# Router of the second norm in each of two encoder layers: from the normed rows to the residual sum, half a tile at a time

## The chip, the cores and the metric

The kernel runs on one core of a Trainium2 chip. The metric is device time in microseconds (us) of one execution, as the median of several runs. Engines are named as in the profile: PE is TensorE (matmul), PEld its weight loads, DVE is VectorE, ACT is ScalarE, POOL is GpSimd, SP is the engine that issues most DMAs.

## The reference

Two post-norm encoder layers on 1024 tokens of width 1024. Only the place around the second norm and the router matters here:

```python
x = layer_norm(DN_ALPHA * x + y, ln2_g[l], ln2_b[l])       # y: cross-attention's output
y = expert_choice_moe(x, moe_router[l], w_gate[l], w_up[l], w_down[l])

def expert_choice_moe(x, w_router, w_gate, w_up, w_down):
    cap = EC_FACTOR * n_tok // N_EXPERTS                   # 128
    aff = jax.nn.softmax((x @ w_router).astype(jnp.float32), axis=-1)   # (tokens, 16)
    gates, idx = lax.top_k(aff.transpose(0, 2, 1), cap)    # each expert takes its 128 best tokens
    xe = jax.vmap(lambda xb, ib: xb[ib])(x, idx)           # gather
    ...                                                    # SwiGLU, scatter-add
```

## The kernel before

Tokens are cut into eight tiles of 128 rows. The function `proj_ln` (L1170 on) does the output projection of cross-attention and the second norm. Its loop (L1188) takes one tile per step `t`; each step has 16 slots `i` of three products (a product of split fp32r halves: high by high, high by low, low by high), 48 products of 512 columns in all. After slot 7 the first half of the row, and after slot 15 the second, is added to the scaled residual (`add`, L1201, on DVE, with the statistics of that half, L1135). Then `layer_norm` (L1138) forms mean and variance (L1144), the root on ACT (L1146), two passes of 1024 columns on DVE (L1148, L1154) and the reciprocal. The normed tile is handed to `emit2`, which writes `x2d` and `yd` to DRAM through ACT's queue.

The router runs as a side thread, a generator `tg` that is moved on at fixed slots. `turned2` transposes the normed tile on PE in two groups of four blocks (L1463), each group is taken out of PSUM by ACT (high part, L175) and DVE (low part, L176); then 16 short products against the router weights `rw` (L1482) give 16 logits twice (for the two parts), ACT copies them (L1484), PE turns them (L1487), DVE adds the two (L1489), and the softmax follows (L1492 to L1497). A tile's two groups are transposed at slots 9 and 10 of the next step, its products come at slot 0 of the step after that and its softmax at slot 6 there.

A second side thread, `bg`, ranks the affinities on DVE: `rank` sorts the scores of four tiles once tile 3's softmax is done, then of two tiles once tile 5's is done. It is moved on by one yield per slot up to slot 8 of the last step, and 11 more yields follow it after the last step, between the pieces of the last tile's router. `route` then ranks the last two tiles (26 yields), with one yield of `bg` behind each of its own as long as `bg` has any; from the threshold it makes two masks, counts tokens by products with a triangle and with ones (L1583 to L1588), and gives every expert its list. Expert 0's rows are gathered (L1651), transposed (L1463), and the first expert product follows. The experts' weights are loaded through SP's queue into a pool of 41 buffers that is shared with everything else.

PE, ACT and DVE execute in the order in which the program is written. SP and POOL are ordered by a planner.

`router_weights` (L1468) loads the 1024 by 16 router weights and splits them; it stands between the last turn of the first norm's rows and the first full products of cross-attention on PE.

Of the kernel before, what the change touches and what calls it, by code (L numbers as in the profile page):

```python
# [11 lines left out]
F32 = mybir.dt.float32  # L12
# [51 lines left out]
R4 = 4  # L64
ST = lambda nc: nc.scalar
YB = 1
EARLY = {4: 1, 5: 2, 6: 2, 7: 6, 8: 5}

FWD = ((0, 2), (4, 6), (1, 3), (5, 7))
# [68 lines left out]
class Net:  # L138
# [58 lines left out]
    def consts(self):  # L197
        nc, cp, A = self.nc, self.cp, self.A
        self.ident = cp.tile([128, 128], F32, name="ident")
        nc.sync.dma_start(self.ident, A["k_ident"])  # L200
        self.eps = cp.tile([128, 2], F32, name="eps")
        nc.vector.memset(self.eps[:, 0:1], 1e-6)
        nc.vector.memset(self.eps[:, 1:2], 1e-5)
        self.x1d = [self.dp.tile([N, D], F32, name=f"x1d{l}") for l in range(DEPTH)]
# [927 lines left out]
    def stats(self, r, st, i):  # L1132
# [2 lines left out]
        self.nc.vector.bn_stats(st[:, i, :], r[:, i * 512:i * 512 + 512])  # L1135
        return st

    def layer_norm(self, r, g, b, split=False, st=None, src=None):  # L1138
# [4 lines left out]
        mv = self.sml(2, "mv")  # L1143
        nc.vector.bn_aggr(mv, st.rearrange("p a b -> p (a b)"))  # L1144
        sd = self.sml(1, "lsd")
        nc.scalar.activation(sd, mv[:, 1:2], AF.Sqrt, bias=self.eps[:, 1:2], scale=1.0)  # L1146
# [23 lines left out]
    def proj_ln(self, raw, ws, res, g, b, emit, turned, per=2, bg=iter(())):  # L1170


        nc = self.nc
        ws[0].get()
        HL = {0: self.split_pair(raw, 0)}
        ws[1].get()
        g = self.bcast(g, 1024, "lng")
        b = self.bcast(b, 1024, "lnb")
        rs = {}

        def load(t):
            rs[t] = self.big(name="r")
            nc.sync.dma_start(rs[t], res[t * 128:(t + 1) * 128, :])

        load(0)
        yield
        done, tg = [], iter(())
        for t in range(NT + 2):  # L1188
            if per == 2:
                tg = turned((t - 3) // 2) if t % 2 and t >= 3 else iter(())  # L1190
            if t < NT:
                if t + 1 < NT:
                    load(t + 1)
                P = [self.psS((128, 512)) for _ in range(2)]
                H, L = HL[t // 2]
                d = slice((t % 2) * 128, (t % 2) * 128 + 128)
                r, st = rs.pop(t), None

                def add(n):
                    c = slice(n * 512, n * 512 + 512)  # L1200
                    nc.vector.scalar_tensor_tensor(r[:, c], r[:, c], ALPHA, P[n], op0=OP.mult, op1=OP.add)  # L1201
                    return self.stats(r, st, n)

                for i in range(16):
                    n, k = divmod(i, 8) if t else (i % 2, i // 2)
# [15 lines left out]
            if per == 2 or t >= NT:  # L1221
# [12 lines left out]
            if t < NT:  # L1234
                for n in range(bool(t), 2):
                    st = add(n)
                self.layer_norm(r, g, b, LS(per, t), st)
                done.append((t, r))
            yield
# [226 lines left out]
            yield  # L1466

    def router_weights(self, l):  # L1468
        nc = self.nc
        raw = self.cp.tile([128, 8, 16], F32, name="rt", tag="rt")  # L1470
        nc.sync.dma_start(raw, self.A["moe_router"][l].rearrange("(k p) e -> p k e", p=128))
        w = self.cp.tile([128, 8, 32], F32R, name="rw", tag="rw")
        self.split(w[:, :, 0:16], w[:, :, 16:32], raw)
        return w

    def router(self, w, X, t):

        nc = self.nc
        P = self.psO((128, 128))
# [4 lines left out]
        nc.scalar.activation(lg[0:32], P[0:32], AF.Copy)  # L1484
        yield
        P = self.psT((128, 2, 16))
        nc.tensor.transpose(P.rearrange("p a e -> p (a e)"), lg[0:32], self.ident[0:32, 0:32])  # L1487
        s = self.sml(16, "rlg")
        nc.vector.tensor_reduce(s, P.rearrange("p a e -> p e a"), axis=AX.X, op=OP.add)  # L1489
        e = self.aff[:, t, 0:16]  # L1490
        nm = self.sml(1, "rnm")
        nc.vector.tensor_reduce(nm, s, axis=AX.X, op=OP.max, negate=True)  # L1492
        sm = self.sml(1, "rsm")
        nc.scalar.activation(e, s, AF.Exp, bias=nm, scale=1.0, accum_out=sm)
# [56 lines left out]
    def route(self, bg):  # L1551
# [28 lines left out]
            nc.vector.tensor_tensor(M[:, j], aff, tb.unsqueeze(1).to_broadcast([128, 8, 16]), op)  # L1580
        C = self.psT((128, 2, 8, 16))
        mm, tri, one = nc.tensor.matmul, self.tri[:, 0, :], self.tri[:, 1, :]
        mm(C, tri, M, start=True, stop=False)  # L1583
# [173 lines left out]
    def run(self):  # L1757
# [38 lines left out]
        for l in range(DEPTH):  # L1796
# [54 lines left out]
            wo2 = []  # L1851
            rw = self.router_weights(l)
            T2 = self.new_T()
            st2 = {}

            def emit2(t, x):
                self.tap(f"x2_{l}_{t}", x)
# [4 lines left out]
                st2[t] = x  # L1862

            def turned2(t):
                X = [self.big((128, 8, 128), F32R, name="xt") for _ in range(2)]
                yield from self.turn_tile(st2.pop(t), *X, TL(t))
                yield from self.router(rw, X, t)
                self.ranked += 1
                yield
# [166 lines left out]
```

## Time and profile before

| what | us |
|---|---|
| median of 3 runs (2730.67 to 2734.1) | 2730.91 |
| the profiled execution | 2730.33 |
| its span, first to last instruction | 2728.6 |

How to read it: the page gives busy time per engine, the chain of work that ended last, and groups of instructions by line. The trace gives rows in order of time: start, duration, engine, line, operation, what is written and read, and in brackets how long the engine was idle before it and what released it. An engine that never waits sets the time of its stretch; an engine that is idle while others are done is waiting on the chain. The stage in question runs from about 930 us to 1077 us for layer 0, and once more for layer 1.

### The profile page before, as it was taken

The page shows a single profiled execution, that of the slowest core. Times are in us where ns is not written, and L with a number is a line of the kernel's source. Part 1 is how long each engine was busy: PE and PEld are TensorE (multiplying, and loading weights), DVE is VectorE, ACT ScalarE, POOL GpSimd, SP SyncE. Part 2 cuts the span into 40 slices and gives each one's busy share as a digit, 9 for nine tenths or more (in the row PEclk, how much of TensorE's full clock was granted, in tenths as well). Part 3 has the DMA queues.
Part 4 walks back from the last instruction along what each step waited for, and adds up shares of the span by engine and source line. Part 5 has one row for each costly group of instructions (what it writes and reads, how often), then busy time and mean ns, then how long its engine had stood idle before and what let it go on. Part 6 is the DMA issues. An engine that isn't in the chain of part 4 may idle for free.

```text
span 2728.6 us, 39209 instructions
## 1 busy us (share of the span) xinstructions
PE 2540.0 (93%) x14132; PEld 2138.4 (78%) x14132; DVE 1963.7 (72%) x3089; ACT 1589.2 (58%) x2828; POOL 830.0 (30%) x761
## 2 busy tenths in 40 slices
PE   7899989999999895999989998999989999599998
PEld 5688879988778784777869887999877888477775
DVE  6765578877645678889876556887765356889887
ACT  4743379988123443887854425998732344377885
POOL 2412427963101201121131333688230130011112
PEclk9899999999999996999999999999999999799999
DMA  7545100333233357999975610005323235699994
GB/s 196 192 161 200 28 24 17 75 100 120 86 109 118 121 187 252 351 378 371 342 241 171 208 60 24 9 24 140 94 85 101 85 101 185 239 340 372 377 344 154
DMA packets 222581, 462.76 MB, mean 170 GB/s; under 512 B 26298, under 2 KB 83216, under 8 KB 222386
## 3 DMA queue, kind: packets, MB, share of 16 engines
q1 hardware_dynamic: 198402, 374.56, 39.2%
q0 software_dynamic: 19376, 68.91, 9.5%
q10 hardware_dynamic: 4608, 16.78, 1.5%
q8 instruction: 111, 1.82, 0.3%
q14 instruction: 84, 0.69, 0.1%
HBM read 369.75 MB, written 90.44 MB: 169 GB/s over the span
## 4 chain that ended last, share of the span: by engine, by line
PE 70%; DVE 13%; issue 5%; ACT 5%; DMA 4%; POOL 2%; SPq 0%; ACTq 0%; DVEq 0%; POOLq 0%
PE S L187 7%; PE S L188 7%; PE S L189 7%; PE S L527 6%; PE O L1709 6%; PE T L544 5%; PE O L189 5%; PE O L188 5%; PE O L187 5%; PE S L421 4%; PE O L555 3%; PE O L554 3%; DVE rk L1512 2%; DMA eg<-moe_w_up 1%; PE T L1463 1%
## 5 line engine op out<-in xcount | busy, mean ns | idle before, releaser
L176 DVE TENSOR_TENSOR egl<-eg,egh 128x1024 fp32r<-128x1024 f32 x256 | 305.8, 1221 | 49.9 <-ACT egh L175 45.6
L530 DVE TENSOR_REDUCE nm<-S 128x1 f32<-128x1024 f32 x192 | 234.5, 1223 | 102.5 <-PE S L527 100.4
L175 ACT ACTIVATE egh<-eg 128x1024 fp32r<-128x1024 f32 x256 | 265.1, 1058 | 41.0 <-PE S L188 23.9
L176 DVE TENSOR_TENSOR PL<-T,PH 128x512 fp32r<-128x512 f32 x384 | 246.3, 683 | 17.4 <-ACT PH L175 14.2
L175 ACT ACTIVATE PH<-T 128x512 fp32r<-128x512 f32 x384 | 209.4, 595 | 69.0 <-PE T L544 67.6
L536 ACT ACTIVATE E<-S,nm 128x1024 f32<-128x1024 f32 x192 | 214.7, 1118 | 7.7 <-DVE nm L530 7.4
L187 PE MATMUL S<-woh,mh 128*128 128x512 f32 x512 | 207.9, 406 | 6.0 <-DVE r L1201 6.0
L544 PE MATMUL T<-ident,E 128*128 128x128 f32 x1536 | 203.4, 274 | 2.3 <-DVE PL L176 1.4
L188 PE MATMUL S<-wol,mh 128*128 128x512 f32 x512 | 202.1, 395 | 3.7 <-POOL wol L176 2.4
L544 PEld LDWEIGHTS T<-ident,E 128*128 128x128 f32 x1536 | 179.7, 141 | 32.2 <-DVE PL L176 4.0
L187 PE MATMUL S<-egh,xt 128*128 128x512 f32 x512 | 204.1, 399 | 0.0
L189 PE MATMUL S<-woh,ml 128*128 128x512 f32 x512 | 201.6, 394 | 0.0
L189 PE MATMUL S<-egh,xt 128*128 128x512 f32 x512 | 200.9, 392 | 0.0
L188 PE MATMUL S<-egl,xt 128*128 128x512 f32 x512 | 200.6, 392 | 0.0
L176 DVE TENSOR_TENSOR edl<-ed,edh 128x1024 fp32r<-128x1024 f32 x128 | 153.2, 1220 | 18.5 <-ACT edh L175 18.5
L1709 PE MATMUL O<-edh,ht 128*128 128x512 f32 x512 | 155.4, 406 | 1.4 <-ACT ht L175 1.4
L527 PE MATMUL S<-KS,QS 128*128 128x512 f32 x512 | 148.1, 413 | 1.6 <-ACT E L536 1.6
L1651 POOL DMA_INDIRECT xg<-x2d,ix x32 | 54.6, 1705 | 301.0 <-PE O L1709 143.0
L175 ACT ACTIVATE edh<-ed 128x1024 fp32r<-128x1024 f32 x128 | 132.4, 1055 | 22.8 <-PE S L188 13.2
L569 POOL TENSOR_TENSOR olo<-olo 64x256 f32<-64x256 f32 x96 | 70.3, 733 | 227.3 <-ACT olo L567 185.3
L554 PE MATMUL O<-PH,VS 128*128 128x256 f32 x512 | 137.9, 302 | 0.0
L1724 POOL DMA_INDIRECT yd<-ye,ix x31 | 49.1, 1583 | 260.9 <-ACT ye L1723 104.8
(438 smaller groups left out, 7093.1 us busy)
## 6 DMA issues: line engine op xcount, KB each, us to landing
eg<-moe_w_gate SPq DMA_DIRECT2D x128, 512.0 KB, 11.2
eg<-moe_w_up SPq DMA_DIRECT2D x128, 512.0 KB, 11.2
ed<-moe_w_down SPq DMA_DIRECT2D x128, 512.0 KB, 11.4
wv<-xa_wkv SPq DMA_DIRECT2D x16, 512.0 KB, 8.0
wk<-xa_wkv SPq DMA_DIRECT2D x16, 512.0 KB, 6.3
wo<-w_o SPq DMA_DIRECT2D x16, 512.0 KB, 3.5
x1d<-r SPq DMA_DIRECT2D x16, 512.0 KB, 2.6
wq<-xa_wq SPq DMA_DIRECT2D x16, 512.0 KB, 4.2
```

Source lines behind the costliest of these rows:

```text
L175: self.nc.scalar.activation(h, src, AF.Copy)
L176: (self.nc.vector if le == "v" else self.nc.gpsimd).tensor_sub(l, src, h.bitcast(F32))
L187: mm(out, ah, bh, start=start, stop=False)
L188: mm(out, ah, bl, start=False, stop=False)
L189: mm(out, al, bh, start=False, stop=stop)
L421: nc.tensor.matmul(P[:, hf * 512:hf * 512 + 512], a[:, k, :], self.half(b, hf, k), start=s, stop=e)
L527: self.nc.tensor.matmul(S[:, hf * 512:hf * 512 + 512], a, b[hf], start=n == 0, stop=n == len(passes) - 1)
L530: self.nc.vector.tensor_reduce(nm, S, axis=AX.X, op=OP.max, negate=True)
L536: self.nc.scalar.activation(E, S, AF.Exp, bias=nm, scale=1.0, accum_out=den)
L544: self.nc.tensor.transpose(pt[:, k, :], P[:, kt * 128:(kt + 1) * 128], self.ident)
L554: nc.tensor.matmul(O[:, :256], v, PH[half][:, k, :], start=kt == 0, stop=False)
L1709: nc.tensor.matmul(O[e][n], a[:, 2 * u + f, :], w[:, n * 512:n * 512 + 512], start=s, stop=z)
```

## The change

- `router_weights` also loads the norm's gain and bias, multiplies the router weights with them on POOL (gain in place, bias into a new tile), and takes the column sums of both over the 1024 inputs with 16 products of 16 columns each whose stationary operand is a 128 by 128 block of ones in fp32.
- The router takes the residual sum `r` in place of the normed row. The two groups are turned at slot 12 of the tile's own step (first half) and at slot 3 of the next step; the products are at slot 6 and the softmax at slot 9 of the next step. The mean and the reciprocal root are brought in afterwards, with two small DVE passes on 16 columns.
- For tiles 4 to 7 the turned rows stay whole fp32 (ACT alone takes them out of PSUM) and eight fp32 products with 16 columns of weights replace 16 split ones. Tiles 0 to 3 keep the split.
- The normed row goes into a tile of its own, `x2`. For the last tile the second pass of the norm stands behind the router's softmax; two yields of `bg` stand in the tail in place of 11.
- In `route` the counting products are seven with the moving operand shifted by a tile (both masks in one), and one over a sum of the first mask, which DVE forms, in place of 14 and 8.

```diff
+RF = lambda t: t >= 4
@@ proj_ln
-                    if per == 1 and i == TK(t)[0]:
-                        tg = turned(t - 1) if t else tg
-                    if per == 1 and i in TK(t) or per == 2 and i % 4 == 3 and t + 1 < NT:
+                    if per == 1 and i == 12 and t:
+                        drain(tg)
+                        tg = turned(t, r)
+                    if per == 1 and (i in (3, 6, 9, 12) and t or i == 2 and t == 1) or per == 2 and i % 4 == 3 and t + 1 < NT:
                         next(tg, None)
...
-            if per == 1 and t == NT:
-                tg = turned(t - 1)
-                for n in BGL:
-                    for _ in range(n):
-                        next(bg, None)
-                    next(tg, None)
-                drain(tg)
             if t < NT:
                 for n in range(bool(t), 2):
                     st = add(n)
+            if per == 1 and t == 0:
+                tg = turned(t, r)
+            if per == 1 and t < NT:
+                x = self.big(name="x2")
+                mv, sd = self.moments(st)
+                rs_ = self.sml(1, "lrs")
+                if t == NT - 1:
+                    next(tg)
+                    nc.vector.reciprocal(rs_, sd)
+                    nc.vector.scalar_tensor_tensor(x, r, mv[:, 0:1], g, op0=OP.subtract, op1=OP.mult)
+                    self.moment[t] = mv, rs_
+                    next(tg)
+                    next(bg, None)
+                    next(bg, None)
+                    drain(tg)
+                    nc.vector.scalar_tensor_tensor(x, x, rs_, b, op0=OP.mult, op1=OP.add)
+                    emit(t, x)
...
@@ router_weights
+        bw = self.tmp((128, 8, 16), name="rbw")
+        nc.gpsimd.tensor_tensor(bw, raw, gb[:, 1].unsqueeze(2).to_broadcast([128, 8, 16]), OP.mult)
+        nc.gpsimd.tensor_tensor(raw, raw, gb[:, 0].unsqueeze(2).to_broadcast([128, 8, 16]), OP.mult)
...
+        P = self.psO((128, 2, 16))
+        for i, x in enumerate((raw, bw)):
+            for k in range(8):
+                nc.tensor.matmul(P[:, i], self.one.to_broadcast([128, 128]), x[:, k], start=k == 0, stop=k == 7)
@@ router
+            if len(X) == 1:
+                nc.tensor.matmul(P[0:16], whole[:, k, :], X[0][:, k, :], start=k == 0, stop=k == 7)
+                continue
...
+        mv, rs = self.moment.pop(t)
+        u = self.sml(16, "rlg")
+        nc.vector.scalar_tensor_tensor(u, c[:, 0], mv[:, 0:1], s, op0=OP.mult, op1=OP.subtract)
+        nc.vector.scalar_tensor_tensor(u, u, rs, c[:, 1], op0=OP.mult, op1=OP.subtract)
@@ route
-        for t in range(NT):
-            for j in range(2):
-                if t < NT - 1:
-                    mm(C[:, j, t + 1:], one, M[:, j, t:t + 1].to_broadcast([128, NT - 1 - t, 16]), start=False, stop=False)
-            mm(C[:, 1], one, M[:, 0, t:t + 1].to_broadcast([128, NT, 16]), start=False, stop=t == NT - 1)
+        for d in range(1, NT):
+            mm(C[:, :, d:], one, M[:, :, 0:NT - d], start=False, stop=False)
+        mm(C[:, 1], one, above.unsqueeze(1).to_broadcast([128, NT, 16]), start=False, stop=True)
```

## Rows read from the trace of the kernel before

**Rows 1.** The page: the chain that ended last, by engine; the 128x512 eviction.
```profile
PE 70%; DVE 13%; issue 5%; ACT 5%; DMA 4%; POOL 2%; SPq 0%; ACTq 0%; DVEq 0%; POOLq 0%
L175 ACT ACTIVATE PH<-T 128x512 fp32r<-128x512 f32 x384 | 209.4, 595 | 69.0 <-PE T L544 67.6
```
**Rows 2.** Busy time by window: PE, PEld, DVE, ACT, POOL, granted clock, DMA share, GB/s.
```profile
1020.00:1035.00 15.00, 14.27 (x77) 11.24 (x76) 13.72 (x50) 5.93 (x11) 0.00 (x0) 1.00 0.78 274
1050.00:1060.00 10.00, 0.00 (x0) 0.00 (x0) 9.74 (x72) 0.00 (x0) 1.56 (x4) 0.50 1.04 402
```
**Rows 3.** Waits of PE from 925 to 1036 us, two lines of three.
```profile
PE S L187 <- DVE r L1201: 0.8, 1, 0.8
PE T L1463 <- DVE rlg L1489: 0.7, 1, 0.7
```
**Rows 4.** Timeline of PE in one undisturbed step: start, duration, engine, line, shapes.
```profile
949.66 0.60 PE L1463 MATMUL T<-ident,r 128*128 128x128 f32 x4
950.01 0.48 PE L187 MATMUL S<-woh,mh 128*128 128x512 f32 x1
...
955.34 1.12 PE L1482 MATMUL O<-xt,rw 128*32 128x128 f32 x16
956.30 0.44 PE L187 MATMUL S<-woh,mh 128*128 128x512 f32 x1
```
**Rows 5.** Whole fp32 products of 512 columns at the end: timeline, then the line's instructions.
```profile
2698.91 1.88 PE L1959 MATMUL S<-r,ident 128*128 128x512 f32 x4
...
L1959 PE MATMUL S<-r,ident x32: 590/592/697, 2695.2 to 2718.0; 128*128 128x512 f32 x32
```
**Rows 6.** Timeline of PE: eight short fp32 products, and the long product behind them.
```profile
810.61 1.03 PE L1403 MATMUL T<-ident,xE 128*128 128x128 f32 x8
811.40 0.48 PE L187 MATMUL O<-xh,wqh 128*128 128x512 f32 x1
```
**Rows 7.** Timeline of the tail of layer 0, from the last projection product on.
```profile
1035.30 1.17 PEld L1482 LDWEIGHTS O<-xt,rw 128*32 128x32 f32 x16
...
1037.51 0.29 ACT L1146 ACTIVATE lsd<-mv,eps 128x1 f32<-128x1 f32 x1 [1.60 <-DVE mv L1144]
1037.71 0.25 ACT L1484 ACTIVATE lg<-O 32x128 f32<-32x128 f32 x1
1037.97 1.28 ACT L1494 ACT_TABLE_LOAD   x1
...
1047.39 0.31 ACT L1494 ACTIVATE aff<-rlg,rnm 128x16 f32<-128x16 f32 x1 [1.09 <-DVE rnm L1492]
...
1048.29 0.24 DVE L1524 STREAM_TRANSPOSE rk<-aff 128x64 f32<-128x64 f32 x1
```
**Rows 8.** Timeline of DVE in the ranking: two threads in turn, then one alone.
```profile
1053.24 1.97 DVE L1512 TENSOR_TENSOR rk<-rk 128x32 f32<-128x32 f32 x16
...
1061.90 1.49 DVE L1512 TENSOR_TENSOR rk<-rk 32x64 f32<-32x64 f32 x8
```
**Rows 9.** Timeline: first counting product, and DVE's first work on the counts.
```profile
1065.14 0.40 PE L1583 MATMUL T<-rM,trib 128*128 128x256 bf16 x1 [0.80 <-DVE rM L1580]
...
1067.20 0.29 DVE L1591 SCALAR_TENSOR_TENSOR rk<-T,rM 128x128 f32<-128x128 f32 x1 [2.12 <-PE T L1588]
```
**Rows 10.** Timeline of DVE: the next pair split, a norm's second pass, a ranking's first step.
```profile
992.53 1.88 DVE L176 TENSOR_TENSOR ml<-xo,mh 128x512 fp32r<-128x512 f32 x3
...
997.81 1.28 DVE L1154 SCALAR_TENSOR_TENSOR r<-r,lrs,lnb 128x1024 f32<-128x1024 f32 x1
...
1002.04 0.31 DVE L1524 STREAM_TRANSPOSE rk<-aff 128x128 f32<-128x128 f32 x1
```
**Rows 11.** The first gather, and DMA by window just before it.
```profile
1070.78 1.04 POOL L1651 DMA_INDIRECT xg<-x2d,ix  x1 [19.01 <-DVE ix L1617]
...
1064.00:1065.00 1.00, 0.28 (x1) 0.17 (x1) 0.59 (x4) 0.00 (x0) 0.00 (x0) 0.50 0.40 152
```
**Rows 12.** SP's queue at the kernel's start: six loads of single values.
```profile
16.55 3.09 SPq L343 DMA_DIRECT2D cw<-hy_conv_w  x6
```

More of the change, by code (lines that the diff above doesn't have):

```diff
@@ L203, in consts @@
         nc.vector.memset(self.eps[:, 1:2], 1e-5)
+        self.one = cp.tile([128, 1], F32, name="one")
+        nc.vector.memset(self.one, 1.0)
         self.x1d = [self.dp.tile([N, D], F32, name=f"x1d{l}") for l in range(DEPTH)]
@@ L1136, in stats, with moments @@
         return st
+    def moments(self, st):
+        mv = self.sml(2, "mv")
+        self.nc.vector.bn_aggr(mv, st.rearrange("p a b -> p (a b)"))
+        sd = self.sml(1, "lsd")
+        self.nc.scalar.activation(sd, mv[:, 1:2], AF.Sqrt, bias=self.eps[:, 1:2], scale=1.0)
+        return mv, sd
     def layer_norm(self, r, g, b, split=False, st=None, src=None):
@@ L1142, in layer_norm @@
             st = self.stats(src, self.stats(src, None, 0), 1)
[L1143 to L1146, printed above, removed]
+        mv, sd = self.moments(st)
         rs = self.sml(1, "lrs")
@@ L1220, in proj_ln @@
                         st = add(0)
-            if per == 2 or t >= NT:
+            if per == 2 or t > NT:
                 drain(tg)
@@ L1236, in proj_ln @@
                     st = add(n)
+            if per == 1 and t == 0:
+                tg = turned(t, r)
+            if per == 1 and t < NT:
+                x = self.big(name="x2")
+                mv, sd = self.moments(st)
+                rs_ = self.sml(1, "lrs")
[10 more added lines that the diff above has]
+                    emit(t, x)
+                else:
+                    nc.vector.scalar_tensor_tensor(x, r, mv[:, 0:1], g, op0=OP.subtract, op1=OP.mult)
+                    nc.vector.reciprocal(rs_, sd)
+                    self.moment[t] = mv, rs_
+                    nc.vector.scalar_tensor_tensor(x, x, rs_, b, op0=OP.mult, op1=OP.add)
+                    done.append((t, x))
+            elif t < NT:
                 self.layer_norm(r, g, b, LS(per, t), st)
@@ L1468, in router_weights @@
     def router_weights(self, l):
-        nc = self.nc
+        nc, A = self.nc, self.A
         raw = self.cp.tile([128, 8, 16], F32, name="rt", tag="rt")
-        nc.sync.dma_start(raw, self.A["moe_router"][l].rearrange("(k p) e -> p k e", p=128))
+        nc.sync.dma_start(raw, A["moe_router"][l].rearrange("(k p) e -> p k e", p=128))
+        gb = self.cp.tile([128, 2, 8], F32, name="rgb", tag="rgb")
+        for i, k in enumerate(("ln2_g", "ln2_b")):
+            nc.sync.dma_start(gb[:, i], A[k][l].rearrange("(k p) -> p k", p=128))
+        bw = self.tmp((128, 8, 16), name="rbw")
+        nc.gpsimd.tensor_tensor(bw, raw, gb[:, 1].unsqueeze(2).to_broadcast([128, 8, 16]), OP.mult)
+        nc.gpsimd.tensor_tensor(raw, raw, gb[:, 0].unsqueeze(2).to_broadcast([128, 8, 16]), OP.mult)
         w = self.cp.tile([128, 8, 32], F32R, name="rw", tag="rw")
         self.split(w[:, :, 0:16], w[:, :, 16:32], raw)
-        return w
+        P = self.psO((128, 2, 16))
+        for i, x in enumerate((raw, bw)):
+            for k in range(8):
+                nc.tensor.matmul(P[:, i], self.one.to_broadcast([128, 128]), x[:, k], start=k == 0, stop=k == 7)
+        c = self.cp.tile([128, 2, 16], F32, name="rc", tag="rc")
+        nc.scalar.activation(c, P, AF.Copy)
+        return w, raw, c
     def router(self, w, X, t):
         nc = self.nc
+        w, whole, c = w
+        n = 16 if len(X) == 1 else 32
         P = self.psO((128, 128))
         for k in range(8):
+            if len(X) == 1:
+                nc.tensor.matmul(P[0:16], whole[:, k, :], X[0][:, k, :], start=k == 0, stop=k == 7)
+                continue
             for a in range(2):
@@ L1483, in router @@
         lg = self.tmp((128, 128), name="lg")
-        nc.scalar.activation(lg[0:32], P[0:32], AF.Copy)
+        nc.scalar.activation(lg[0:n], P[0:n], AF.Copy)
         yield
[L1486 to L1489, printed above, removed]
+        P = self.psT((128, n))
+        nc.tensor.transpose(P, lg[0:n], self.ident[0:n, 0:n])
+        if n == 16:
+            s = P
+        else:
+            s = self.sml(16, "rlg")
+            nc.vector.tensor_reduce(s, P.rearrange("p (a e) -> p e a", a=2), axis=AX.X, op=OP.add)
+        mv, rs = self.moment.pop(t)
+        u = self.sml(16, "rlg")
+        nc.vector.scalar_tensor_tensor(u, c[:, 0], mv[:, 0:1], s, op0=OP.mult, op1=OP.subtract)
+        nc.vector.scalar_tensor_tensor(u, u, rs, c[:, 1], op0=OP.mult, op1=OP.subtract)
         e = self.aff[:, t, 0:16]
         nm = self.sml(1, "rnm")
-        nc.vector.tensor_reduce(nm, s, axis=AX.X, op=OP.max, negate=True)
+        nc.vector.tensor_reduce(nm, u, axis=AX.X, op=OP.min)
         sm = self.sml(1, "rsm")
-        nc.scalar.activation(e, s, AF.Exp, bias=nm, scale=1.0, accum_out=sm)
+        nc.scalar.activation(e, u, AF.Exp, bias=nm, scale=-1.0, accum_out=sm)
         ri = self.sml(1, "rri")
@@ L1582, in route @@
         mm, tri, one = nc.tensor.matmul, self.tri[:, 0, :], self.tri[:, 1, :]
+        above = self.tp.tile([128, 16], BF16, tag="olo", name="rab", bufs=2)
+        with nc.allow_low_precision("counts up to 8"):
+            nc.vector.tensor_reduce(above, M[:, 0].rearrange("p t e -> p e t"), axis=AX.X, op=OP.add)
         mm(C, tri, M, start=True, stop=False)
-        for t in range(NT):
-            for j in range(2):
-                if t < NT - 1:
-                    mm(C[:, j, t + 1:], one, M[:, j, t:t + 1].to_broadcast([128, NT - 1 - t, 16]), start=False, stop=False)
-            mm(C[:, 1], one, M[:, 0, t:t + 1].to_broadcast([128, NT, 16]), start=False, stop=t == NT - 1)
+        for d in range(1, NT):
+            mm(C[:, :, d:], one, M[:, :, 0:NT - d], start=False, stop=False)
+        mm(C[:, 1], one, above.unsqueeze(1).to_broadcast([128, NT, 16]), start=False, stop=True)
         yield
@@ L1853, in run @@
             T2 = self.new_T()
-            st2 = {}
+            self.moment = {}
             def emit2(t, x):
@@ L1861, in emit2, with turned2 @@
                 ST(nc).dma_start(self.yd[l][t * 128:(t + 1) * 128, :], y)
[L1862 to L1866, printed above, removed]
+            def turned2(t, r):
+                if RF(t):
+                    X = [self.big((128, 8, 128), name="xt")]
+                    for c in range(2):
+                        pt = self.psT((128, 4, 128))
+                        for k in range(4):
+                            j = c * 4 + k
+                            nc.tensor.transpose(pt[:, k, :], r[:, j * 128:(j + 1) * 128], self.ident)
+                        nc.scalar.activation(X[0][:, c * 4:c * 4 + 4, :], pt, AF.Copy)
+                        yield
+                else:
+                    X = [self.big((128, 8, 128), F32R, name="xt") for _ in range(2)]
+                    yield from self.turn_tile(r, *X, TL(t))
                 yield from self.router(rw, X, t)
```

## The prediction, made before the changed kernel was run

> **What bounds the kernel now.** I read the chain of waits first: by engine PE has 70% of it and DVE 13% [rows 1]. So in most stages an instruction added on PE is paid, and the stage around this change may be one of the DVE stretches. The windows tell the two apart. From 1020 to 1035 us, inside the last projection steps, PE is busy 14.27 of 15 us at the full clock, and DVE 13.72 of 15: PE ends last, with DVE close behind. From 1050 to 1060 PE does nothing, the granted clock is 0.50 and DVE is busy 9.74 of 10 [rows 2]. So a step lasts as long as its PE work, and from the last projection product until the lists are made, the chain is the router of tile 7, then the ranking on DVE, then the counts. The timeline of that tail gives its parts: last product 1035.30, ranking of tiles 6 and 7 from 1048.29 [rows 7], counting products from 1065.14 [rows 9], gather 1070.78 [rows 11]. The waits say how far PE already waits for DVE in the steps: 0.8 and 0.7 us [rows 3], little beside eight steps. Layer 1 repeats all of it, so each term below is paid twice.
>
> **A. Column sums, on PE.** New work where PE runs without a pause, at the start of cross-attention. Each fp32 product appears as two records: the 16 products of 512 columns on the last stage are 32 records [rows 5]. So 16 products are 32 records, each with a 128-column fp32 stationary and 16 moving columns. No row has that shape. The nearest is eight fp32 records with 128 stationary and 128 moving columns, which hold PE 0.79 us, 0.10 each [rows 6]; 32 of them are 3.2, with 0.1 of fill **+3.3**. Bounds: the sixteen router records take 0.96, 0.06 each [rows 4], so 1.9; above, 0.12 each if the short stream hides nothing of a load, 3.9. POOL's multiplications, the extra small evictions and DVE's column pass lie long before they are used; I cost them at nothing. Without that cover they would delay the first router, by under 1 us.
>
> The row shows 0.10 per record with 128 moving columns, which doesn't tell whether the stationary or the moving side sets it. [...]
>
> **B. PE work ahead of the last projection product.** Tiles 4, 5 and 6 now have their fp32 products inside the steps; before, the split products of tiles 4 and 5 were there and tile 6's came behind the last product. An fp32 record of 512 columns takes (1.88 - 0.59) / 3 = 0.43 [rows 5], so one of 128 columns 0.1075, and a tile, eight products, 16 records, 1.72. A split tile takes 0.96 [rows 4]. 3 x 1.72 - 2 x 0.96 = 3.24; one more group's fill and turn of logits, 0.5 (an estimate from the 0.35 that four transposes take [rows 4]); the first half of tile 7 turned before the end, 0.35 and 0.1 of fill. **+4.2**. The bounds are 0.06 per record (then 0.96 a tile, +1.9) and 4.7.
>
> **C. DVE and the slots.** The first ranking starts when tile 3's softmax is through: now at 1002.04, in step 5 [rows 10]; after the change at slot 9 of step 4, the step in which DVE also splits halves of the next pair (1.88) [rows 10]. DVE's row sum then comes late, and the second half of tile 4, turned at slot 3, waits at PE, behind which the projection's products are queued: about 1.5 (an estimate: half of DVE's added 3 us is taken up by slots that have slack). For tiles 0 to 3 the products wait for the low half that DVE makes only three slots earlier; 0.2 a tile, 0.8. Of the 1.5 of waits now [rows 3] I take off 1.1, as the reasons shift but part recurs. **+1.2**. Bounds: -1.1 (no new wait) and +3 (the whole of DVE's addition).
>
> **D. Last product to ranking: 13.0 now** (1048.29 - 1035.30) [rows 7]. After: the root starts 2.2 behind the product as now and ends at 2.5 [rows 7]; ACT takes the second half out of PSUM, 0.6 [rows 1], 3.1; fp32 products 1.72 with a small fill, 4.9; logits 0.25, 5.2; then the table load, 1.28 [rows 7], under which the turn and the small DVE passes lie, 6.4; from the exponential to the ranking 0.9 [rows 7], 7.3; and the second pass of the norm, 1.28 [rows 10], ahead of it on DVE, 8.6. **-4.3**. What goes is the wait for the whole normed row before the turns, and nine yields of the other ranking. Bounds: -2.6 if the clock is already at half for the fp32 products (1.72 more), -4.8 if ACT takes the half out ahead of the root.
>
> **E. Ranking.** Where two rankings take turns DVE does 16 operations in 1.97, where one is alone 8 in 1.49 [rows 8]: two operations a yield cost 0.25 beside another and 0.37 alone, the rest hidden delay. By my count of yields 18 of the other thread are left beside this one, not 22: four fewer pairs of 0.54, four more of 0.37, **-0.7** (0 to -1.2). **F. Counts.** 23 products of 2176 columns lie in 2.06 us at the half clock [rows 9]; 1280 columns in nine products: **-0.7** (-0.3 to -0.9). DVE's sum over the tiles lies beside the first products.
>
> **Other.** Two more loads of single values at the kernel's start, each like one of the six (0.5) [rows 12], on SP ahead of others: +0.3 once, at most 1. Tile 7's normed row is written 1.3 us later, still ahead of the gather. SP's load of layer 1's router weights now waits for layer 0's last fp32 router, and SP's later loads stand behind it; those are hundreds of microseconds ahead of use.
>
> **The sum.** 3.3 + 4.2 + 1.2 - 4.3 - 0.7 - 0.7 = +3.0 a layer, 6.0 for two, and 0.3: +6.3 on the profiled 2730.33, 2736.6. The median is 0.6 above that execution, so **2737**, +0.2%. About 0.2%, 5.5 us, is what a measurement of this kernel can tell from no change; the forecast lies at that bound.
>
> **Rivals.** *One: short fp32 records are cheap.* If 16 and 128 moving columns cost 0.06 as the router's records do [rows 4], A is 1.4 and B 2.3 less, -0.7 a layer, **2730**; with C at its low end 2725. For it: the router's records overlap their loads. Against: eight fp32 records at 0.10 [rows 6]. It decides if 16 records of a router take under 1.2 us. Chance 0.30. *Two: the gather meets the weights.* The chain is shorter by 5.7, so the gather starts about 29.8 us behind the last product; the loads of the experts' weights end at about 1064.4, 29 behind it (402 GB/s at 1050, 0.40 share in 1064 to 1065) [rows 2, 11]. If their buffers come free only some microseconds later, because the extra tile `x2` holds one, gather and loads share the DMA engines; a gather that waits for 3.5 more adds 7: **2744**, up to 2750. It decides where loads are still above a share of 0.8 at the gather. Chance 0.12, slower. *Three: the steps have room.* If DVE's split of late tiles, 0.6 twice a tile, was what ended steps, B and C are not paid in full: -2.5 to -5 a layer, **2718 to 2726**. For it: DVE 13.72 of 15; against: PE 14.27 and 1.5 of waits [rows 2, 3]. Chance 0.13. *That it doesn't do what it says*, a late tile held up for want of a buffer, lies in two.
>
> **Chances.** The forecast case (2733 to 2742) 0.45, split by the bound into 0.28 slower and 0.17 same; one 0.30 (0.20 same, 0.10 faster); two 0.12 slower; three 0.13 faster. Faster 0.23, same 0.37, slower 0.40. The forecast's own range is 2733 to 2742; for 8 in 10, with rival one in it and parts of two and three, 2724 to 2745.
>
> **What would show it.** A: 32 records between the last turn of the first norm and the next full product; over 3 us or under 2. B: spacing of a late tile's 16 router records, 1.7 or under 1.2. C: PE's wait for the row sum ahead of tile 4's second turn. D: last product to the ranking's first transposition 8.6. F: 1.3 us of counts. Rival two: the DMA share when the gather is issued. I am wrong if the last product comes less than 4 us later in its stage, or if D is above 10.

## The result and the profile after

The changed kernel takes 2755.81 us (median of four runs, 2753.56 to 2757.26) against 2732.51 for the kernel before on the same occasions: a ratio of 1.0083 (95% interval 1.0066 to 1.0101), slower by some 23 us. The prediction said 2737, with 2745 as the upper end of the range. The profiled execution took 2756.14 us, its span is 2754.4.

To see where the time went I put equal instructions of both traces side by side, in order, and followed by how much those of after come later. The shift is 1.2 us ahead of layer 0's column sums and 8.0 behind them; 16.9 at the last projection product; 13.2 at the first expert product. In layer 1 it is 14.3, 21.1, 29.7 and 25.6 at the same places. So each layer pays three times and gets back once. Some 2.5 us of the 25.8 in the span arise elsewhere, in stretches that the change doesn't touch. Such shifts come and go between the traces of the experiments below (the 1.2 ahead of layer 0's sums stands in e3_rank_late and e7_presum_later, and not in e1_presum, e2_own_rt and e5_wide), so they are not laid to the change.

**The sums.** The timeline of PE in the changed kernel, around the column sums, and busy time by window (PE, PEld, DVE, ACT, POOL, granted clock, DMA share, GB/s):

```profile
789.71 1.86 PE L1511 MATMUL O<-rt,one 128*128 128x16 f32 x16
791.42 3.18 PE L1511 MATMUL O<-rbw,one 128*128 128x16 f32 x16
794.44 0.77 PE L188 MATMUL O<-xh,wqh 128*128 128x512 f32 x1
795.01 0.63 PE L189 MATMUL O<-xl,wqh 128*128 128x512 f32 x1
795.44 0.63 PE L190 MATMUL O<-xh,wql 128*128 128x512 f32 x1
...
790.00:792.00 2.00, 2.00 (x20) 2.00 (x19) 1.43 (x3) 0.71 (x2) 0.00 (x0) 0.96 0.00 0
792.00:794.00 2.00, 2.00 (x11) 2.00 (x11) 0.00 (x0) 0.00 (x0) 0.00 (x0) 0.50 0.00 0
794.00:796.00 2.00, 2.00 (x7) 1.71 (x8) 0.00 (x0) 0.20 (x1) 0.00 (x0) 0.50 0.00 0
796.00:798.00 2.00, 2.00 (x7) 1.52 (x6) 0.00 (x0) 0.00 (x0) 0.00 (x0) 0.50 0.00 0
798.00:800.00 2.00, 2.00 (x9) 1.65 (x8) 0.00 (x0) 0.00 (x0) 0.00 (x0) 0.83 0.00 0
```

The first sixteen records run at a granted clock of 1.00 and take 1.71 us, 0.107 each. Then the granted clock falls from 1.00 to 0.50, though PE is busy in all of each window. The second sixteen take 3.02, 0.19 each, and the full products behind them stand 0.43 apart, where 0.23 is usual, until about 798.6. That is 6.8 us in place of 3.3.

**The stage.** First and last projection product of layer 0 in the kernel before (the row at 1035.30 in [rows 7], which I took for the last product, is the router's weight load that starts 0.01 us behind it), then in the changed kernel with some rows between. The last fence has PE's waits in the changed kernel (engine, line, what it waited for: us in total, times, longest); of its first line, 0.8 is tile 7's second half, behind the last projection product:

```profile
930.57 0.60 PE L187 MATMUL S<-woh,mh 128*128 128x512 f32 x1
...
1035.29 0.39 PE L189 MATMUL S<-woh,ml 128*128 128x512 f32 x1
```
```profile
939.11 0.39 PE L188 MATMUL S<-woh,mh 128*128 128x512 f32 x1
...
1007.92 0.39 PE L190 MATMUL S<-woh,ml 128*128 128x512 f32 x1
1010.70 1.12 PE L1923 MATMUL T<-ident,r 128*128 128x128 f32 x4 [2.40 <-DVE r L1208]
1011.47 0.78 PE L188 MATMUL S<-woh,mh 128*128 128x512 f32 x1
1012.04 0.63 PE L189 MATMUL S<-wol,mh 128*128 128x512 f32 x1
...
1014.74 1.92 PE L1524 MATMUL O<-xt,rt 128*16 128x128 f32 x16
1016.59 0.50 PE L188 MATMUL S<-woh,mh 128*128 128x512 f32 x1
...
1052.14 0.40 PE L190 MATMUL S<-woh,ml 128*128 128x512 f32 x1
```
```profile
PE T L1923 <- DVE r L1208: 3.2, 2, 2.4
PE S L188 <- DVE r L1208: 1.0, 1, 1.0
```

The stage is 113.0 us long, 104.7 before. Two things are to be seen. A late tile's sixteen fp32 records take 1.85 us (1014.74 to 1016.59), much as forecast. And ahead of tile 4's second turn PE stands for 2.4 us behind DVE's row sum; the products after it are 0.43 to 0.57 apart: here, too, the granted clock is 0.50 behind the wait (0.57 as the mean from 1010 to 1014, the wait's end included).

**The tail, the counts and the gather** in the changed kernel, in order of time; these answer to [rows 7], [rows 9] and [rows 11]:

```profile
1052.58 0.69 DVE L1208 SCALAR_TENSOR_TENSOR r<-r,S 128x512 f32<-128x512 f32 x1 [3.16 <-PE S L190]
...
1053.90 2.24 PE L1524 MATMUL O<-xt,rt 128*16 128x128 f32 x16
...
1054.47 0.58 ACT L1924 ACTIVATE xt<-T 128x512 f32<-128x512 f32 x1
1056.18 0.27 ACT L1529 ACTIVATE lg<-O 16x128 f32<-16x128 f32 x1 [1.14 <-PE O L1524]
...
1059.73 0.24 DVE L1576 STREAM_TRANSPOSE rk<-aff 128x64 f32<-128x64 f32 x1
...
1075.88 0.40 PE L1638 MATMUL T<-rM,trib 128*128 128x256 bf16 x1 [0.80 <-DVE rM L1632]
1077.24 0.29 DVE L1644 SCALAR_TENSOR_TENSOR rk<-T,rM 128x128 f32<-128x128 f32 x1 [1.13 <-PE T L1641]
...
1080.81 1.04 POOL L1704 DMA_INDIRECT xg<-x2d,ix  x1 [3.32 <-DMA eg<-moe_w_up]
1088.45 1.94 PE L1489 MATMUL T<-ident,xg 128*128 128x128 f32 x8 [7.71 <-DMA xg<-x2d,ix]
```

From the last product to the ranking 7.6 us (13.0 before), from there to the counts 16.15 (16.85), the counts 1.36 (2.06): all that was to be gained came, and more. But the gathered rows are turned 7.6 us after the gather was issued, where it took 4.5 in the kernel before (gather in [rows 11]; turn at 1075.29). The windows say why that may be: from 1080 to 1088 the DMA engines' share is 1.03 to 1.05 at some 400 GB/s, and the kernel before had none of that load left at its gather (issued at 1070.78 [rows 11]; the first line is a window of the kernel before). SP's queue in the changed kernel shows one place where the weights were held up:

```profile
1071.00:1072.00 1.00, 0.00 (x0) 0.00 (x0) 0.09 (x1) 1.00 (x3) 0.82 (x1) 0.50 0.00 0
```
```profile
1023.68 0.37 SPq L128 DMA_DIRECT2D eg<-moe_w_up  x1
1056.18 0.37 SPq L1499 DMA_DIRECT2D rt<-moe_router  x1
1056.64 0.53 SPq L128 DMA_DIRECT2D eg<-moe_w_gate  x1
```

SP issues nothing from 1024 to 1056: it stands on the load of layer 1's router weights, which waits for tile 7's fp32 products (they end at 1056.14), and all weights behind it wait too.

### The profile page after: what moved, and what is told of

Its sections match the earlier page's. It is cut to its first block, busy times and chain, and to the rows that moved or that the text cites. A ratio compares the mean times of both kernels' runs of the same rounds, so it can differ in the third digit from the quotient of the medians.

```text
span 2754.4 us, 39304 instructions
## 1 busy us (share of the span) xinstructions
PE 2560.4 (93%) x14168; PEld 2152.4 (78%) x14168; DVE 1964.1 (71%) x3100; ACT 1596.6 (58%) x2834; POOL 834.3 (30%) x765
## 6 DMA issues: line engine op xcount, KB each, us to landing
eg<-moe_w_gate SPq DMA_DIRECT2D x128, 512.0 KB, 11.2
```

## The experiments

Each is an edit of the changed kernel. "Stage" is from the first to the last projection product, "tail" from there to the first counting product, "gather" from its issue to the turn of its rows; layer 0, then layer 1. With four runs of a kernel the interval of its ratio to the kernel before is some 0.18% to either side, 5 us, and the changed kernel was not run again beside the experiments. So a median that differs from the changed kernel's by less than that tells nothing by itself, and the readings rest on stretches of the traces.

| kernel | median, us | before beside it | stage | tail | gather |
|---|---|---|---|---|---|
| before | | | 104.7, 104.7 | 29.9, 29.9 | 4.5, 4.4 |
| changed | 2755.8 | 2732.5 | 113.0, 113.3 | 23.7, 23.8 | 7.6, 7.1 |
| e1_presum | 2746.1 | 2730.9 | 111.7, 113.3 | 23.7, 23.7 | 7.9, 7.0 |
| e5_wide | 2744.2 | 2730.9 | 113.3, 113.3 | 23.7, 23.7 | 7.7, 7.0 |
| e7_presum_later | 2740.9 | 2731.8 | 111.7, 113.3 | 23.7, 23.7 | 7.7, 6.9 |
| e3_rank_late | 2748.0 | 2730.9 | 109.1, 109.2 | 25.7, 25.3 | 7.9, 5.3 |
| e11_pool_split | 2751.5 | 2731.6 | 113.3, 113.3 | 23.7, 23.9 | 7.9, 7.1 |
| e4_one_fp32 | 2754.6 | 2731.8 | 113.7, 113.7 | 23.7, 23.7 | 8.1, 6.5 |
| e2_own_rt | 2751.1 | 2730.9 | 113.1, 113.3 | 23.7, 23.7 | 7.1, 6.2 |
| e6_inplace | 2754.2 | 2731.8 | 113.3, 113.3 | 23.7, 23.7 | 7.9, 7.0 |
| e10_fewer_loads | 2752.1 | 2731.6 | 113.3, 113.3 | 23.7, 23.8 | 7.7, 4.6 |
| e8_all | 2737.4 | 2731.8 | 112.6, 112.8 | 25.3, 25.3 | 5.2, 4.6 |
| e13_best | 2728.6 | 2731.3 | 109.1, 109.2 | 24.3, 24.3 | 4.6, 4.4 |
| e14_best_late | 2731.2 | 2731.3 | 109.1, 109.1 | 25.3, 25.4 | 4.6, 4.6 |

### The column sums and the clock

e1_presum sums on DVE first; then one product takes the place of sixteen:

```diff
-            for k in range(8):
-                nc.tensor.matmul(P[:, i], self.one.to_broadcast([128, 128]), x[:, k], start=k == 0, stop=k == 7)
...
+            nc.vector.tensor_reduce(cs[:, i], x.rearrange("p k e -> p e k"), axis=AX.X, op=OP.add)
+        nc.tensor.matmul(P, self.one.to_broadcast([128, 128]), cs, start=True, stop=True)
```

> One part of the change made cheap: DVE first sums the router weights over the eight blocks, and one product of 32 columns takes the place of the sixteen of 16 columns (2 records in place of 32 per layer). Theory one (the run of 32 short records costs 3.4 us at the full clock and makes the granted clock fall to 0.50, which costs as much again): the clock stays at 1.00 behind the sums, full products keep 0.23 us each, and 6.4 us a layer come back, 12 to 13 in all, about 2743. Rival (the clock falls there anyway, since PE was idle for 1.1 us ahead of the sums): the clock still falls, 3 us a layer come back, about 2750.

9.7 us came back, between the two; across the sums themselves it is 2.5 a layer. PE in layer 0:

```profile
790.06 0.58 PE L1512 MATMUL O<-rcs,one 128*128 128x32 f32 x2 [2.16 <-DVE rcs L1511]
790.44 0.78 PE L188 MATMUL O<-xh,wqh 128*128 128x512 f32 x1
```

The sixteen short products are gone, but PE, in order, now waits 2.16 us for DVE's sums, and the clock is down behind that wait (0.54 as the mean from 790 to 792). The run doesn't tell the theories apart: the clock fell behind a wait that the changed kernel doesn't have.

e5_wide keeps all sixteen products and their stationary operand, and lets each move 128 columns, the same 16 eight times:

```diff
-        P = self.psO((128, 2, 16))
+        P = self.psO((128, 2, 8, 16))
...
-                nc.tensor.matmul(P[:, i], self.one.to_broadcast([128, 128]), x[:, k], start=k == 0, stop=k == 7)
+                nc.tensor.matmul(P[:, i], self.one.to_broadcast([128, 128]), x[:, k].unsqueeze(1).to_broadcast([128, 8, 16]), start=k == 0, stop=k == 7)
```

> The sixteen products stay, with the same stationary block of ones, but each moves 128 columns (the same 16 eight times) in place of 16. Theory one in the form 'few moving columns make the clock fall': the records stay at 0.11 to 0.12 us and the clock stays at 1.00 or falls later, the 32 records take 3.4 to 3.8 us, and 3 us a layer come back, about 2750. Rival ('fp32 stationary loads of 128 columns make it fall, whatever moves'): the clock falls as before and the time is that of the change within 2 us, 2754 to 2757.

```profile
785.23 1.26 PE L253 MATMUL T<-ident,r 128*128 128x128 f32 x8 [1.13 <-DVE xl L177]
786.32 1.95 PE L1511 MATMUL O<-rt,one 128*128 128x128 f32 x16
788.11 1.95 PE L1511 MATMUL O<-rbw,one 128*128 128x128 f32 x16
789.82 0.47 PE L188 MATMUL O<-xh,wqh 128*128 128x512 f32 x1
...
788.00:790.00 2.00, 2.00 (x20) 2.00 (x19) 0.04 (x1) 0.00 (x0) 0.00 (x0) 1.00 0.00 0
790.00:792.00 2.00, 2.00 (x11) 1.64 (x10) 0.00 (x0) 0.20 (x1) 0.00 (x0) 1.00 0.00 0
```

This tells the theories apart. Eight times the columns and the same 32 records: 1.79 and 1.71 us, 0.11 each, and the clock stays at 1.00 in both layers though the same wait of 1.13 stands ahead. The shift across the sums falls by 3.2 us in either layer (the median by 11.6; the rest lies in stretches far from the sums). So at a granted clock of 1.00 a record with 128 stationary columns took 0.107 to 0.112 here, whether 16 or 128 columns moved. (That its moving side is free doesn't follow: the late routers' records, 16 stationary and 128 moving columns, take 0.116.) As for the clock, neither the 32 loads nor the wait, nor both together, were enough in this run to make it fall. With 16 moving columns it fell among the second sixteen records in all 14 cases (both layers of the changed kernel and of the six experiments that leave the sums alone), with 128 in neither of two.

e7_presum_later emits the one product a section later, so that PE need not wait:

```diff
...
             for n, _ in enumerate(cross):
+                if n == 0:
+                    self.sums()
```

> As the run that first sums on DVE, with the one product a section of cross-attention later, so that PE doesn't wait for DVE's sums. Theory one: neither a wait nor a fall of the clock between 786 and 800 us, the whole price of the column sums (6.8 a layer) but 0.3 comes back, 13 in all, 2743. Rival (the clock falls there anyway, or DVE's two reductions make later work wait): at least 2 us a layer stay, 2747 or more.

14.9 us came back. The shift across the place is 6.5 us less in either layer, the clock is 1.00 in each window from 786 to 796, and there is no wait on the sums. The sums as written cost 6.8 a layer; they can be had for 0.3.

The traces of e1_presum and e7_presum_later hold one more thing, further on in layer 0. The wait of 2.4 us ahead of tile 4's second turn is there as in the changed kernel, but the clock stays at 1.00 behind it. In e1_presum:

```profile
1005.91 0.66 PE L1924 MATMUL T<-ident,r 128*128 128x128 f32 x4 [2.39 <-DVE r L1208]
1006.33 0.47 PE L188 MATMUL S<-woh,mh 128*128 128x512 f32 x1
...
1006.00:1008.00 2.00, 2.00 (x11) 1.73 (x12) 1.93 (x3) 0.78 (x2) 0.00 (x0) 1.00 1.03 398
```

Their stage is 111.7 there, against 113.3 in their layer 1, where the clock does fall. So of the 4 us that this place costs, some 2.4 are the wait and 1.6 the clock behind it. The fall is not certain: it came in 16 of the 18 cases in which PE stood for 2.3 to 2.4 us at this place, and what spared the other two stays open.

### The wait ahead of tile 4's second turn

e3_rank_late doesn't move the first ranking on in step 4:

```diff
-BG = lambda t, i: t < 7 or i < 9
+BG = lambda t, i: t != 4 and (t < 7 or i < 9)
```

> The first ranking isn't moved on in step 4, so it starts in step 5 as in the kernel before. Theory three (DVE's ranking and its split of the next pair together make the row sum late; PE waits 2.4 us for it ahead of tile 4's second turn, and the granted clock falls to 0.50 behind that wait): the wait falls under 0.5, the clock stays at 1.00 through step 5, 3 to 4 us a layer come back ahead of the last product; about seven more yields of the first rankings lie beside the last one and give 1 to 2 of it back, about 2751. Rival (the DVE work is only moved): PE waits as long for tile 5's second turn, under 1 us in all.

```profile
PE S L188 <- DVE r L1208: 1.0, 1, 1.0
PE T L1923 <- DVE r L1208: 0.8, 1, 0.8
```

The wait of 2.4 is gone (0.8 is left, ahead of tile 7's second half), the clock stays at 1.00 from 1006 to 1014, and the stage is 3.9 and 4.1 us shorter. 1.6 to 1.9 of it is given back in the tail, as forecast; in layer 0 the gather meets the weights as before. Median: 7.8 less.

e11_pool_split leaves the ranking and takes DVE's part of the split away instead: POOL makes all four low halves of that pair, by a flag passed from step 4.

```diff
-            self.split(H[jp // 2][:, d, :], L[jp // 2][:, d, :], raw[hf][jp][:, :, c], SPP(jp))
+            self.split(H[jp // 2][:, d, :], L[jp // 2][:, d, :], raw[hf][jp][:, :, c], "p" if pool else SPP(jp))
```

> In step 4 POOL makes all four low halves of the next pair, not one of four (1.88 us less on DVE there); the first ranking still starts in step 4. Theory three (ranking and split together make the row sum late): PE's wait ahead of tile 4's second turn falls from 2.4 to under 0.8 and the clock stays at 1.00, the stage from 113 to 109.5 us, and no yield moves into the tail, so 3.5 us a layer, 7 in all, about 2749. Rival (the ranking alone is enough to make the sum late): the wait stays over 1.5 us and the clock falls.

The wait is 2.3 and the stage is as long as in the changed kernel. DVE and POOL in step 4 of that run, and the same operations of DVE in the changed kernel:

```profile
1002.84 5.00 POOL L177 TENSOR_TENSOR ml<-xo,mh 128x512 fp32r<-128x512 f32 x4 [23.75 <-DVE rk L1584]
...
1004.63 2.08 DVE L1559 TENSOR_TENSOR rk<-rk 128x64 f32<-128x64 f32 x2
1006.74 1.32 DVE L1564 TENSOR_TENSOR rk<-rk 128x64 f32<-128x64 f32 x2
```
```profile
1006.56 1.29 DVE L1559 TENSOR_TENSOR rk<-rk 128x64 f32<-128x64 f32 x2
1007.88 0.36 DVE L1564 TENSOR_TENSOR rk<-rk 128x64 f32<-128x64 f32 x2
```

The run doesn't show that ranking alone is enough, as the rival has it: the 1.88 us that left DVE came back as longer operations of its own. Pairs that take 0.36 alone take 1.3 to 2.1 while POOL works on the split (looked at one by one, three of the four operations end 0.08 us after one of POOL's four does), and even in the changed kernel one pair takes 1.29 beside POOL's one quarter (1006.34 to 1007.63).

e4_one_fp32 splits tiles 4 to 6 as the early ones:

```diff
-RF = lambda t: t >= 4
+RF = lambda t: t >= 7
```

> Only tile 7 keeps whole fp32 rows; tiles 4 to 6 are split as tiles 0 to 3 are. Theory: PE has three routers of 0.96 in place of 1.85 us, 2.7 us a layer ahead of the last product, and DVE gets six low halves of 0.68 back, which lie in its slack in steps 5 and 7 and lengthen PE's waits by 1 at most: 3 to 5 us less in all, about 2752. Rival (DVE is the end of those steps): PE's waits grow by as much as it saved, under 1 us in all.

The rival: the stage is 113.7, no shorter. PE saves 0.9 on each of three routers and waits 3.1 us for low halves from DVE, which it hardly did (0.2). Whole fp32 rows cost nothing net here: without them PE saves 2.7 and waits 2.9 more for DVE.

### The gather

e2_own_rt loads the router weights through ACT's queue, early in their own layer:

```diff
+    def router_load(self, l):
+        raw = self.cp.tile([128, 8, 16], F32, name="rt", tag="rt")
+        self.nc.scalar.dma_start(raw, self.A["moe_router"][l].rearrange("(k p) e -> p k e", p=128))
+        return raw
```

> Layer 1's router weights are loaded through ACT's queue, early in layer 1, and no longer through SP's. Theory two (SP stood from 1024 to 1056 us on that load, which waited for layer 0's last fp32 router, and the experts' weights behind it came late and met the gather): SP's gap is gone, the loads are through before the first gather of layer 0, which lands in 4.4 us as before and not in 7.6: 3 us less in layer 0, nothing in layer 1, about 2752.5. Rival (the loads wait for the buffer of the last normed row in any case, as in layer 1, where no router weights are loaded): the gather of layer 0 still takes 7 us or more, under 1 us in all.

SP's gap is gone, but layer 0's gather still takes 7.1: as the rival says. The weights now stand one place later, on a buffer:

```profile
1051.44 9.72 SPq L128 DMA_DIRECT2D ed<-moe_w_down  x2
1061.25 0.61 SPq L128 DMA_DIRECT2D eg<-moe_w_gate  x1
```

That load goes on just after the write of the last normed row has landed (issued 1058.12, 2.6 us to landing). In the changed kernel the same load goes on after 1067.5, where that write landed. (The median is 4.7 lower; of that, 0.6 lies at the first gather and 0.9 at the second. Another 1.9 is there before layer 0's sums, where the edit has nothing to do with it.)

e6_inplace gives the last normed row no tile of its own:

```diff
-                x = self.big(name="x2")
+                x = r if t == NT - 1 else self.big(name="x2")
```

> The last tile's normed row goes into the tile of its residual sum, as in the kernel before, so the stage takes one buffer of the pool less per layer. Theory four (the experts' weights come later because their buffers come free later, and one of those is the extra tile): the loads of the weights end earlier against the last product, the gather lands in 4.4 to 6 us in place of 7 to 7.6, 1 to 3 us a layer less, about 2752. Rival (the order in which buffers go round counts, not their number): gather as long as now, within 1 us of the change.

7.9 and 7.0: the rival. One buffer more or less isn't it.

e10_fewer_loads asks for ten loads less in the last step; they stand behind the first gather:

```diff
-EARLY = {4: 1, 5: 2, 6: 2, 7: 6, 8: 5}
+EARLY = {4: 1, 5: 2, 6: 2, 7: 6}
```

> The ten loads of experts' weights that are asked for in the last step stand behind the first gather in the program; nothing else differs from the changed kernel. Theory two and four in their common form (the gather is slow because weights are still coming through the same 16 DMA engines): fewer weights move when the gather is issued, the gather lands in 4.4 to 5 us in place of 7.1 to 7.6, 2.5 to 3 us a layer less; the first experts may then wait for weights and give some back, 2750 to 2754. Rival (the gather is slow for another reason, the late write of the last row or the rows' addresses): it lands in 7 us as now.

It is split between the layers, and that is what makes it plain. Windows around layer 1's gather, in this run (issued 2398.45) and in the changed kernel (issued 2400.54):

```profile
2398.00:2400.00 2.00, 0.38 (x7) 0.29 (x5) 0.60 (x3) 1.71 (x7) 1.25 (x2) 0.50 0.29 114
2400.00:2402.00 2.00, 0.00 (x0) 0.00 (x0) 2.00 (x3) 1.57 (x2) 1.79 (x1) 0.50 0.84 242
```
```profile
2400.00:2402.00 2.00, 0.47 (x8) 0.38 (x7) 0.51 (x3) 1.71 (x8) 1.16 (x2) 0.50 1.02 400
2402.00:2404.00 2.00, 0.00 (x0) 0.00 (x0) 2.00 (x2) 1.67 (x2) 1.88 (x1) 0.50 1.04 390
```

In layer 1 the weights are through, the share is 0.29 at the issue, and the rows are there in 4.6 us; nothing is given back by the experts (against the changed kernel the shift goes from -2.1 to -4.9 at this gather and in the first products behind it, and stays there until 2717). In layer 0, where SP still stands 32 us on the router weights, even the smaller number of loads is late, the share is 1.0, and the gather takes 7.7. So the meeting with the weights is the cause, and it has two sources: SP's wait (layer 0 alone) and the chain being shorter than the loads (both). Neither repair alone frees layer 0's gather (7.1 in e2_own_rt, 7.7 here); e13_best below, with both and a tail that is 0.6 longer, has 4.6 there.

### All together

e8_all joins the sums of e7, the load of e2, the late ranking of e3, the split of e4 and the tile of e6.

> All at once: sums first on DVE with the one product later, layer 1's router weights through ACT's queue, the first ranking kept out of step 4, only tile 7 as whole fp32, its normed row in the tile of its sum. If the theories add up: per layer -6.5 (sums), -3.7 (wait and clock ahead of tile 4's turn), -2.7 (routers), -2 (gather), +2 (yields that move into the last ranking): 13 a layer, 26 in all, 2730, the time of the kernel before. Rival (the gather's meeting with the weights takes up what the chain gains): 2735 to 2740.

2737.4, the rival's time, though not for the rival's reason: the gathers take 5.2 and 4.6. It is e4's part that spoils it: the stage is 112.6 where e3 alone has 109.1, with 4.9 us of PE's waits for low halves.

e13_best and e14_best_late leave that out, and e6, and put the loads of e10 in. They differ in the yields of the first ranking in step 4: three or none.

```diff
-BG = lambda t, i: t < 7 or i < 9
+BG = lambda t, i: t < 7 and (t != 4 or i < 12) or i < 9
```

> The repairs that worked, together, on the changed kernel with tiles 4 to 7 as fp32: sums first on DVE with one product later, layer 1's router weights through ACT's queue, the ten late loads of weights behind the first gather, and three of the seven yields of the first ranking left in step 4. If the causes add up, per layer against the kernel before: sums 0.3, stage 4.5 to 5, last product to counts -5.5, counts -0.7, gather 0 to 0.3: -1 a layer, and the time 2727 to 2732, not distinguishable from the kernel before or a little under it. Rival (something of the 25 us is still not named): 2735 or more.

> As the run beside it, but with no yield of the first ranking in step 4. The wait ahead of tile 4's second turn is then 0.8 or less for certain, the stage 109.1, and last product to counts 25.5 (1.8 more than the changed kernel, from the yields that move into the tail): 0 to 1 us a layer more than the run beside it if three yields fit into step 4, 3 us a layer less if they don't.

e13_best: 2728.6 against 2731.3, ratio 0.9994 (0.9985 to 1.0003); e14_best_late 2731.2, 1.0003 (0.9994 to 1.0012). Neither can be told from the kernel before, as expected: with the sums, the wait and the gather mended, the loss is gone. Three yields fit into step 4 (the stage is 109.1 in both), and the tail is 1.0 shorter with them.

## Why the prediction was wrong

Most of the loss lies in three steps: the column sums, priced without the clock; DVE's lateness, taken at under a third of its size; and the gather, taken at nothing. By the prediction's own terms, per layer (two numbers: layer 0, layer 1):

| term | forecast | measured |
|---|---|---|
| A column sums | +3.3 | +6.8, +6.8 |
| B work on PE ahead of the last product | +4.2 | +4.4, +4.4 (stage of e13_best less that of before) |
| C DVE late for PE | +1.2 | +4.0, +4.1 (stage of the change less that of e13_best) |
| D last product to ranking | -4.3 | -5.4, -5.4 |
| E ranking | -0.7 | -0.7 |
| F counts | -0.7 | -0.7 |
| gather | 0 | +3.1, +2.7 |
| sum | +3.0 | +11.5, +11.2 |

From ahead of the sums to the first expert product the shift grows by 12.0 and 11.3; the half a microsecond over in layer 0 arises between the sums and the stage.

**A** failed on the clock. The spacing was right to a hundredth (0.10 forecast, 0.107 measured), and so was the choice of [rows 6] as the nearest row. What was missing is that those rows move 128 columns and the new ones 16: no bound asked what a run of such records does to the granted clock, and at 0.50 most of the second half of them and 4 us of products behind were paid nearly twice (0.19 a record against 0.107, 0.43 from product to product against 0.23). The upper bound of 3.9 was a bound on spacing alone.

**B and F** came out as worked out. The fp32 router's 1.85 against 1.72 I lay to the fill, which no run tests. **E** is partly luck: its 0.54 for two pairs in turn isn't what [rows 8] gives (1.97 for eight pairs, so 0.49 for two), and with 0.49 the term is -0.5; it measured -0.7.

**C** had the right mechanism, place and tile, and the wrong size: the wait was 2.4, not 1.5, and behind it the clock fell again, 1.6 more, which made 4.0 and 4.1 in all, beyond the upper bound of 3. The small parts offset one another: the 0.8 for low halves of tiles 0 to 3 was one wait of 0.2, and of the 1.5 of waits before, 1.3 is still there in e13_best (this lies in B as measured). That "half of DVE's addition is taken up by slack" was not read from any row; [rows 2] (DVE 13.72 of 15) spoke against it.

**D** was better than forecast by 1.1, beyond its lower bound: the first half's eight records run while ACT is still taking the second half out of PSUM (products from 1053.90, the eviction at 1054.47), where I had put all sixteen behind it.

**The gather** was rival two, held at 0.12 and priced at 3.5 a layer; it took 3.1 and 2.7. The prediction had the two numbers side by side (gather 29.8 us behind the last product, loads through at 29) and still gave it little weight. The reason that it gave, the buffer of the extra tile, was not it (e6_inplace). Its worst sentence is the one that cleared SP's queue: that the loads behind layer 1's router weights are hundreds of microseconds ahead of use. Layer 1's router weights are; layer 0's expert weights, queued behind them, were wanted at once. The step asked when the waiting load is needed, and not when those behind it are. (With that wait alone taken away, in e2_own_rt, the gather was only 0.6 shorter and still met the weights.) The late write of the last row, called "still ahead of the gather", mattered in the same way: not for the gather, but for a weight that waits for its buffer.

Rivals one and three, both on the fast side, found nothing for them: records cost 0.107 and 0.116, and B was paid in full.

The two signs that the prediction named for being wrong did not come up: the last product came 8.3 us later in its stage, and D was 7.6. The first watches for a stage that gains too little length, the second for a tail that stays too long; none watches for sums or a stage that cost too much, or for a slower gather.

## What to carry to other kernels

Price a new stretch of short products twice: by its spacing, and by what the granted clock does during and behind it; the long products behind a short stretch pay for a lapse of the clock that came in it (here 0.43 us apart in place of 0.23, for 4 us). When a chain in the tail gets shorter, look at what used to be finished by its end, and when a load gains a wait, list the loads behind it on its queue with their own due times. And a cheaper chain is no gain while its price is laid on the engine that bounds the stage: here e13_best, with the three losses repaired, wins 6.2 us a layer from the last product to the gather and pays 4.7 of them on PE, and the 1.5 that remain a layer can't be told from nothing in its time.

## What the runs showed of the hardware

- PE was busy through whole windows of 2 us while the granted clock fell: 32 fp32 records with a 128-column stationary and 16 moving columns went with a fall from 1.00 to 0.50 behind the first sixteen (14 of 14 cases); with 128 moving columns, 0.11 a record against 0.107, it stayed at 1.00 (e5_wide, 2 of 2).
- Behind a wait of PE of 2.3 to 2.4 us in a full stream of long products the clock fell to 0.50 in 16 of 18 cases and cost 1.6 us more; in the other two it stayed at 1.00.
- Pairs of DVE's ranking operations (128x64) took 1.3 to 2.1 us beside a TENSOR_TENSOR of POOL, 0.36 without it (changed kernel, e11_pool_split); in e11_pool_split three of the four ended 0.08 us after one of POOL's. Moving the split from DVE to POOL gained nothing there: the wait was 2.3 us against 2.4, the stage 113.3 against 113.0 and 113.3.
- A gather of 128 rows took 4.4 to 4.6 us where the DMA engines' share was 0 to 0.5 about its issue, and 7 to 8 where weights kept them at 1.0 throughout.
